# A transformer hybrid on one core: the first layer's shift vector summed on the tensor engine

## The chip, the core and the metric

The kernel runs on one core of a Trainium2 chip, as one launch. The metric is the device time of one execution in us. Matmuls run on the tensor engine (PE; its weight loads are the row PEld), elementwise work on the vector engine (DVE), activations and casts on ScalarE (ACT), small transfers and fills are issued by GpSimd (POOL), large transfers by SyncE (SP). SBUF is the working memory, PSUM holds the sums of the matmuls.

## The reference, cut to what matters

The network has 256 tokens of 1024 numbers, two layers of one kind (mixer, then a feed-forward or an expert stage) and two more of another. Each half of a layer begins with a normalised x, scaled and shifted by vectors which depend on one condition vector c alone. The change concerns the very first of these:

```python
def modulation(c, w, b):
    m = jnp.einsum("bd,de->be", jax.nn.silu(c), w) + b
    shift, scale, gate = jnp.split(m, 3, axis=-1)
    return shift[:, None], scale[:, None], gate[:, None]
...
    x = layer_norm(x, ln0_g, ln0_b)
    for layer in range(DEPTH):
        shift, scale, gate = modulation(c, ada_w[layer, 0], ada_b[layer, 0])
        ...
```

Shift, scale and gate are each a product of one row of 1024 numbers with a 1024 x 1024 matrix of float32, 4 MB from HBM.

## The kernel before

**Front.** Constants and x are loaded, x is normalised row by row in two tiles of 128 tokens (`layer_norm`, L436 to L448, mostly ScalarE, with short steps on the vector engine), and transposed by the tensor engine in blocks of 128x128 (`make_h`, L486). Meanwhile the modulation's first two vectors are made: `fill` takes them one after the other from a plan, scale first. `mod_rows` (L274) loads two row blocks of 128 x 1024 in one transfer of 1 MB and the vector engine multiplies each with its number of silu(c) per partition and adds it to a running tile `macc` (L292 for the first, L294 for the others): eight passes per vector. `mod_done` (L296) then sums `macc` over the partitions with eight matmuls against a column of ones (L171 is the line of the helper `mm`) and the vector engine adds the bias (L327). `ab` (L509) makes columns A and B of scale and shift with the first norm's gain and bias; ScalarE and the vector engine bring the transposed tokens through `x A + B` (L503, L501), cast them to their high part (L505) and take the rest as the low part (L506).

**Products.** Each product is made of three matmuls with exact high and low parts (L166, L167, L168). Weights come in blocks of 1 MB (`raw`, L119, issued by SP, four buffers), are cast by ScalarE (`hi`, L147) and subtracted on the vector engine (`lo`, L148). The first mixer begins with two projections (`proj_nat`, L605) and goes on with convolution, scan, attention, gating.

**What sets the order.** The program is written stage by stage; a scheduler places each engine's instructions in one fixed order, in which the engine then takes them, waiting at each for its inputs. A tile's buffer is taken again when its last reader is done: a transfer into one of the four `raw` buffers waits for that, and transfers issued behind it by SP wait with it.

**Small operands.** `setup` (L335) stacks vectors row by row into tiles (`stack`, transfers issued by POOL), transposes each stack on the tensor engine and copies it (`columns`, L379): col3 with the modulation's biases, col1 with the norms' gains, col2 and col4 with the rest.

## Time and profile before

| what | value |
|---|---|
| time, median of 3 runs | 2099.36 us (2097.38 to 2099.42) |
| span of the profiled execution, first to last instruction | 2100.0 us |
| its own time by the profile | the span: the page gives no other |
| busy: PE, PEld, DVE, ACT, POOL | 93%, 80%, 79%, 58%, 2% |
| mean granted clock of the tensor engine | 0.968 |
| HBM read, mean rate | 552.19 MB, 263 GB/s |

The shares are means over all stages. The front, in which the change lies, is 45 us of the span, and there the tensor engine is mostly idle. A timeline row gives start, duration, engine, line, operation, result and operands, how many instructions were merged into the row, and in brackets how long the engine was idle before and what ended it.

### The profile page before, as it was taken

What the parts mean: (1) busy time and instruction counts of PE and PEld (TensorE: products, weight loads), DVE (VectorE), ACT (ScalarE), POOL (GpSimd) and SP (SyncE); (2) the same over time, 40 slices, a digit from 0 to 9 for tenths busy, and PEclk for the clock granted to TensorE, in tenths of its full rate; (3) what the DMA queues carried; (4) which work ended last, traced back from release to release, by engine and by line L of the source; (5) the groups of instructions that cost most, each with busy time, mean ns of one, the idle gap of its engine ahead of it and who ended that gap; (6) DMA issues with size and microseconds to landing.
All of it is one profiled execution on the core that took longest, in us unless ns stands there. A gap on an engine that the chain in (4) does not pass through costs nothing.

```text
span 2100.0 us, 30041 instructions
## 1 busy us (share of the span) xinstructions
PE 1959.5 (93%) x11481; PEld 1681.4 (80%) x11481; DVE 1658.0 (79%) x2512; ACT 1208.3 (58%) x1817; POOL 50.1 (2%) x98
## 2 busy tenths in 40 slices
PE   3998999898599999999999999969989999998999
PEld 3887999886478787878778887858869998978998
DVE  6888977897588888888888888889778877667554
ACT  3454444452378767767776777755454446545442
POOL 4000000100000000000000000000000000000000
PEclk9999999998599999999999999979999999999999
DMA  9585998565489999899989999958339894326662
GB/s 319 181 287 202 339 331 308 177 224 204 141 300 360 328 339 334 317 358 346 340 322 348 344 360 351 360 181 278 124 132 346 322 320 147 121 87 214 203 199 80
DMA packets 283238, 555.25 MB, mean 264 GB/s; under 512 B 10172, under 2 KB 137520, under 8 KB 283088
## 3 DMA queue, kind: packets, MB, share of 16 engines
q1 hardware_dynamic: 280000, 549.49, 74.6%
q0 software_dynamic: 2656, 3.20, 0.8%
q8 instruction: 91, 1.49, 0.3%
q10 hardware_dynamic: 432, 0.58, 0.1%
q14 instruction: 59, 0.48, 0.1%
HBM read 552.19 MB, written 1.05 MB: 263 GB/s over the span
## 4 chain that ended last, share of the span: by engine, by line
PE 64%; DVE 5%; ACT 2%; issue 1%; DMA 1%; ACTq 0%; DVEq 0%
PE pp L167 12%; PE pp L168 11%; PE pp L166 11%; PE pa L634 6%; PE ya L167 4%; PE ya L166 4%; PE ya L168 4%; PE pp L175 3%; PE pj L166 1%; PE pj L167 1%; PE pj L168 1%; PE pp L171 1%; DVE lo L148 1%; PE sa L171 1%; ACT hi L147 1%
## 5 line engine op out<-in xcount | busy, mean ns | idle before, releaser
L148 DVE TENSOR_TENSOR lo<-raw,hi 128x1024 fp32r<-128x1024 f32 x660 | 787.5, 1220 | 193.1 <-ACT hi L147 191.5
L147 ACT CAST hi<-raw 128x1024 fp32r<-128x1024 f32 x660 | 668.4, 1051 | 393.6 <-PE pp L167 157.9
L166 PE MATMUL pp<-h,hi 128*128 128x256 f32 x960 | 274.4, 286 | 0.0
L168 PE MATMUL pp<-h,lo 128*128 128x256 f32 x960 | 271.6, 283 | 0.0
L167 PE MATMUL pp<-h,hi 128*128 128x256 f32 x960 | 271.5, 283 | 0.0
L148 DVE TENSOR_TENSOR lo<-rawx,hi 128x1024 fp32r<-128x1024 f32 x176 | 208.5, 1220 | 42.4 <-ACT hi L147 42.3
L294 DVE SCALAR_TENSOR_TENSOR macc<-raw,const,macc 128x1024 f32<-128x1024 f32 x168 | 215.3, 1281 | 6.6 <-DMA raw<-in_ada_w_dram 2.3
L167 PEld LDWEIGHTS pp<-h,hi 128*128 128x128 f32 x960 | 184.1, 192 | 1.9 <-issue 1.2
L166 PEld LDWEIGHTS pp<-h,hi 128*128 128x128 f32 x960 | 184.0, 192 | 1.8 <-ACT hi L147 1.0
L168 PEld LDWEIGHTS pp<-h,lo 128*128 128x128 f32 x960 | 184.1, 192 | 0.0
L147 ACT CAST hi<-rawx 128x1024 fp32r<-128x1024 f32 x176 | 176.5, 1048 | 11.9 <-PE pp L168 9.9
L166 PE MATMUL pj<-hi,h 128*128 128x256 f32 x576 | 169.6, 295 | 8.2 <-ACT h L505 3.7
L167 PE MATMUL pp<-lo,h 128*128 128x512 f32 (+1 forms) x480 | 174.6, 364 | 1.2 <-DVE lo L148 1.0
L166 PE MATMUL pp<-hi,h 128*128 128x512 f32 (+1 forms) x480 | 173.0, 361 | 0.0
L167 PE MATMUL pj<-lo,h 128*128 128x256 f32 x576 | 166.0, 290 | 0.8 <-DVE lo L148 0.8
L168 PE MATMUL pj<-hi,h 128*128 128x256 f32 x576 | 165.9, 290 | 0.0
L634 PE MATMUL pa<-hi,s 128*128 128x512 f32 x528 | 151.5, 396 | 0.0
L167 PE MATMUL pp<-lo,xe 128*128 128x512 f32 (+1 forms) x384 | 146.5, 382 | 1.3 <-DVE lo L148 1.0
L166 PE MATMUL pp<-hi,xe 128*128 128x512 f32 (+1 forms) x384 | 145.2, 379 | 0.0
L168 PE MATMUL pp<-hi,xe 128*128 128x512 f32 (+1 forms) x384 | 144.7, 377 | 0.0
L168 PE MATMUL pp<-hi,x 128*128 128x512 f32 (+1 forms) x384 | 143.2, 373 | 0.0
L167 PE MATMUL ya<-lo,s 128*128 128x512 f32 x352 | 141.9, 403 | 0.0
(481 smaller groups left out, 3563.3 us busy)
## 6 DMA issues: line engine op xcount, KB each, us to landing
raw<-in_moe_w_dram SPq DMA_DIRECT2D x176, 1024.0 KB, 6.1
rawx<-in_moe_w_dram SPq DMA_DIRECT2D x88, 1024.0 KB, 6.5
raw<-in_ada_w_dram SPq DMA_DIRECT2D x48, 1024.0 KB, 6.9
raw<-in_w_mod_dram SPq DMA_DIRECT2D x48, 1024.0 KB, 6.3
raw<-in_w_in_dram SPq DMA_DIRECT2D x42, 1024.0 KB, 5.8
raw<-in_ffn_w_dram SPq DMA_DIRECT2D x33, 1024.0 KB, 6.1
raw<-in_w_gate_dram SPq DMA_DIRECT2D x22, 1024.0 KB, 5.4
raw<-in_w_up_dram SPq DMA_DIRECT2D x22, 1024.0 KB, 5.5
```

Source lines behind the costliest of these rows:

```text
L147: self.nc.scalar.copy(h, v[:, z:z + m])
L148: self.nc.vector.tensor_tensor(l, v[:, z:z + m], h.bitcast(F32), ALU.subtract)
L166: mm(out, lhsT=a[0], rhs=b[0], start=start, stop=False)
L167: mm(out, lhsT=a[0], rhs=b[1], start=False, stop=False)
L168: mm(out, lhsT=a[1], rhs=b[0], start=False, stop=stop)
L171: self.nc.tensor.matmul(out, lhsT=lhsT, rhs=rhs, start=start, stop=stop)
L175: self.nc.tensor.transpose(out, in_, self.ident[:p, :p])
L294: V.scalar_tensor_tensor(acc, v[:, i], c, acc, ALU.mult, ALU.add)
L634: mm(accs[t][h], lhsT=y[ia][:, s], rhs=W[ib][:, h * 512:(h + 1) * 512], start=start and ia == 0 and ib == 0, stop=stop and ia == 1)
```

## The change

The shift vector of the first layer no longer goes over the vector engine. A new function `mod_first` loads its row blocks by turns with the scale's; each 128x128 piece of a shift block is the stationary operand of a matmul with one moving column, silu(c) for that row block, and all sums stay in one PSUM tile, which a matmul with zeros has opened. The last two row blocks of the shift come in transfers of their own, with the scale's sum between them. Around it: the gain columns col1 are made in the middle of `mod_first`, all other setup columns after `make_h` of the first step (in a PSUM pool of that stage; the stacks now have tiles of their own); the transposes of the first step are given a higher priority in the scheduler; the first gate's blocks are issued after the last matmul of the second projection. Comments and docstrings were also removed, which moves line numbers.

```diff
     def mm3(self, out, a, b, start, stop):
-        mm = self.nc.tensor.matmul
+        mm = self.mm_
...
+    def mm_(self, *args, **kw):
+        self.pe_last = self.nc.tensor.matmul(*args, **kw)
...
                 if key in self.gates_pe:
-                    self.mod_gate_pe(key)
+                    with self.tc.issue_after(self.pebar):
+                        self.mod_gate_pe(key)
...
+    def mod_first(self, scale, shift, setup):
+        w, b, j, c0 = self.mod_src(shift)
+        wv = w.rearrange("(k p) n -> p k n", p=128)
+        p = self.ps()
+        self.mm(p[:, 0:KD], self.zero, self.zero[:, 0:KD], True, False)
+        def shift_rows(k0, n):
+            v = self.raw(wv[:, k0:k0 + n, j * D:(j + 1) * D])
+            for i in range(n):
+                c = self.csil[:, c0 + k0 + i:c0 + k0 + i + 1]
+                for q in range(KD):
+                    self.mm(p[:, q:q + 1], v[:, i, q * 128:(q + 1) * 128], c, False, k0 + i == KD - 1 and q == KD - 1)
+        for k in range(0, KD, 2):
+            self.modpos = k
+            self.mod_rows(scale)
+            if k < 6:
+                shift_rows(k, 2)
+            else:
+                shift_rows(k, 1)
+                next(setup)
+                self.mods[scale] = self.mod_done(scale)
+                shift_rows(k + 1, 1)
+        c = self.tl("col", [128, KD])
+        q = ((shift[0] * 2 + shift[1]) * 3 + j) * KD
+        self.nc.vector.tensor_tensor(c, p[:, 0:KD], self.col3[:, q:q + KD], ALU.add)
+        self.mods[shift] = c
...
-            r = self.sc([128, 128])
+            r = self.tl("const", [128, 128], tag="r" + tag)
...
-            p = self.ps()
+            p = self.ps(pool="pp" if "pp" in self.pools else "sd")
...
         self.col1 = columns("col1", *r1)
+        yield
         self.col2 = columns("col2", r2, q)
...
-                for j in range(4):
-                    k = q + j
-                    self.tr(p[:, j], xn[:, t, k * 128:(k + 1) * 128])
+                with self.tc.high_priority(offset=400) if self.step == 1 else nullcontext():
+                    for j in range(4):
+                        k = q + j
+                        self.tr(p[:, j], xn[:, t, k * 128:(k + 1) * 128])
...
         p1 = self.proj_nat(h, w, 1448)
+        self.pebar = self.pe_last.ins
...
-            self.mod_start(plan[0])
+            self.mod_start([])
             x = self.load_x(a["x"])
             xn = x = self.layer_norm(x)
-            self.fill(KD * KD)
-            for _ in setup:
-                pass
+            self.mod_first((0, 0, SC), (0, 0, SH), setup)
...
                     h = self.make_h(xn, A, B)
+                    for _ in setup:
+                        pass
```

On the tensor engine, between the first transposes of the tokens and the first product, stood before (x_149 are the normalised tokens, const_103 the unit matrix, const_105 the ones, macc_204 and macc_232 the running tiles of scale and shift, sh_119, sh_126 and sh_144 the stacks col1, col2, col4; a row counts matmuls as they were written; each one-column matmul of float32 is two passes in the trace):

```order
L175 MATMUL pa_343<-const_103,x_149 128x128 x4
L175 MATMUL pa_355<-const_103,x_149 128x128 x4
L175 MATMUL pa_367<-const_103,x_149 128x128 x4
L171 MATMUL pp_222<-const_105,macc_204 128x1 x8
L171 MATMUL pp_250<-const_105,macc_232 128x1 x8
L175 MATMUL pp_260<-const_103,sh_119 128x112
L175 MATMUL pp_264<-const_103,sh_126 128x94
L175 MATMUL pp_268<-const_103,sh_144 128x96
L175 MATMUL pa_379<-const_103,x_149 128x128 x4
L166 MATMUL pj_423<-hi_415,h_341 128x256
```

and stands now (const_111 is silu(c), pp_204 the shift's sums, the raw tiles its row blocks, const_119, const_126 and const_144 the stacks):

```order
L178 MATMUL pp_287<-const_103,const_119 128x112
L178 MATMUL pa_374<-const_103,x_149 128x128 x4
L178 MATMUL pa_386<-const_103,x_149 128x128 x4
L174 MATMUL pp_204<-const_111,raw_211 128x1 x16
L178 MATMUL pa_398<-const_103,x_149 128x128 x4
L174 MATMUL pp_204<-const_111,raw_233 128x1 x16
L174 MATMUL pp_204<-const_111,raw_255 128x1 x16
L174 MATMUL pp_204<-const_111,raw_277 128x1 x8
L174 MATMUL pp_292<-const_105,macc_206 128x1 x8
L174 MATMUL pp_204<-const_111,raw_302 128x1 x8
L178 MATMUL sd_422<-const_103,const_126 128x94
L178 MATMUL sd_426<-const_103,const_144 128x96
```

The two sums of eight matmuls have become five groups of 16 or 8 for the shift with the scale's sum before the last of them; three of the four groups of transposes keep their place ahead, col1 moved ahead of them all, and the other stacks behind the sums.

On the vector engine, at the start, stood before (const_272 and const_274 are constants, const_117 is col3, t_150 to t_153 belong to the first token tile's mean and variance):

```order
L400 CAST const_272<-const_103 128x128
L403 CAST const_274<-const_103 128x128
L379 COPY const_117<-pp_115 128x96
L404 CAST const_274<-const_103 128x128
L443 TENSOR_SCALAR t_151<-t_150 128x1
L445 TENSOR_SCALAR t_153<-t_152 128x1
```

and stands now (const_430 is such a constant, const_289 is col1):

```order
L434 CAST const_430<-const_103 128x128
L412 COPY const_117<-pp_115 128x96
L412 COPY const_289<-pp_287 128x112
L477 TENSOR_SCALAR t_151<-t_150 128x1
L479 TENSOR_SCALAR t_153<-t_152 128x1
L185 TENSOR_SCALAR t_159<-t_153 128x1
```

The copy of col1 from pp_287 came in between col3 and the first step of the mean (t_151).

On ScalarE, from the end of the normalisation to the casts of the second or first weight block, stood before (hi_415 and hi_419 are the first block's halves; dc and h tiles are the tokens' parts, pa the transposes):

```order
L448 ACTIVATE x_149<-x_146,t_181,t_200 128x1024
L147 CAST hi_415<-raw_413 128x1024
L147 CAST hi_419<-raw_413 128x1024
L503 ACTIVATE dc_344<-pa_343,col_338,col_336 128x128 x3
L503 ACTIVATE dc_356<-pa_355,col_338,col_336 128x128 x2
L505 CAST h_341<-dc_344 128x4x128
L503 ACTIVATE dc_356<-pa_355,col_338,col_336 128x128
L503 ACTIVATE dc_368<-pa_367,col_338,col_336 128x128 x3
L505 CAST h_341<-dc_356 128x4x128
L503 ACTIVATE dc_380<-pa_379,col_338,col_336 128x128
L505 CAST h_341<-dc_368 128x4x128
```

and stands now (hi_465 and hi_469 are the first block's halves):

```order
L482 ACTIVATE x_149<-x_146,t_181,t_200 128x1024
L538 ACTIVATE dc_375<-pa_374,col_369,col_367 128x128 x3
L538 ACTIVATE dc_387<-pa_386,col_369,col_367 128x128 x2
L540 CAST h_372<-dc_375 128x4x128
L538 ACTIVATE dc_387<-pa_386,col_369,col_367 128x128
L538 ACTIVATE dc_399<-pa_398,col_369,col_367 128x128 x3
L540 CAST h_372<-dc_387 128x4x128
L538 ACTIVATE dc_411<-pa_410,col_369,col_367 128x128
L540 CAST h_372<-dc_399 128x4x128
L538 ACTIVATE dc_411<-pa_410,col_369,col_367 128x128 x2
L147 CAST hi_465<-raw_463 128x1024
L540 CAST h_372<-dc_411 128x4x128
```

The first weight block's two casts went from ahead of the tokens' steps to behind most of them.

## Rows read from the trace of the kernel before

**Rows 1.** The page's chain that ended last, share of the span by engine
```profile
PE 64%; DVE 5%; ACT 2%; issue 1%; DMA 1%; ACTq 0%; DVEq 0%
```

**Rows 2.** Waits of the tensor engine, 45 to 185 us; us in total, times, longest
```profile
PE pp L175 <- DVE x L562: 3.7, 1, 3.7
PE pp L175 <- ACT x L558: 3.1, 1, 3.1
```

**Rows 3.** Timeline of the front (start, us, engine, line, operation, count)
```profile
1.45 0.63 POOL L259 DMA_DIRECT2D gate<-in_ada_b_dram  x1
...
4.60 0.50 POOL L370 DMA_DIRECT2D sh<-in_norm_ffn_dram  x1
...
6.84 0.42 PE L175 MATMUL pp<-const,sh 96*128 96x96 f32 x1 [1.93 <-DMA sh<-in_ada_b_dram]
...
7.30 0.26 DVE L379 COPY const<-pp 128x96 f32<-128x96 f32 x1 [2.56 <-PE pp L175]
...
7.61 0.15 DVE L443 TENSOR_SCALAR t<-t 128x1 f32<-128x1 f32 x1
...
12.40 1.97 PE L175 MATMUL pa<-const,x 128*128 128x128 f32 x8 [5.14 <-ACT x L448]
...
26.24 0.74 DVE L292 TENSOR_SCALAR macc<-raw,const 128x1024 f32<-128x1024 f32 x1
...
27.02 9.21 DVE L294 SCALAR_TENSOR_TENSOR macc<-raw,const,macc 128x1024 f32<-128x1024 f32 x7
...
33.59 1.99 ACT L147 CAST hi<-raw 128x1024 fp32r<-128x1024 f32 x2 [12.40 <-DMA raw<-in_w_in_dram]
...
36.28 3.57 PE L171 MATMUL pp<-const,macc 128*128 128x1 f32 x16 [10.16 <-DVE macc L294]
...
42.42 0.16 DVE L521 TENSOR_TENSOR col<-col,col 128x8 f32<-128x8 f32 x1
```

**Rows 4.** Timeline at the first token tiles and products, 42 to 50 us
```profile
42.67 1.85 ACT L503 ACTIVATE dc<-pa,col,col 128x128 f32<-128x128 f32 x5 [7.09 <-DVE col L521]
...
45.10 0.57 PE L166 MATMUL pj<-hi,h 128*128 128x256 f32 x1
...
46.83 0.41 PE L166 MATMUL pj<-hi,h 128*128 128x256 f32 x1
...
47.04 0.41 PE L167 MATMUL pj<-lo,h 128*128 128x256 f32 x1
...
48.31 0.28 PE L167 MATMUL pj<-lo,h 128*128 128x256 f32 x1
...
48.35 1.10 ACT L147 CAST hi<-raw 128x1024 fp32r<-128x1024 f32 x1
...
48.43 0.28 PE L168 MATMUL pj<-hi,h 128*128 128x256 f32 x1
...
49.48 1.23 DVE L148 TENSOR_TENSOR lo<-raw,hi 128x1024 fp32r<-128x1024 f32 x1 [0.52 <-ACT hi L147]
```

**Rows 5.** Timeline of the tensor engine in the routing stage
```profile
548.96 6.84 PE L171 MATMUL pp<-sh,h 128*128 128x8 f32 x32
```

**Rows 6.** Timeline of the tensor engine where one-column and 256-column passes alternate
```profile
140.35 0.28 PE L171 MATMUL pa<-const,macc 128*128 128x1 f32 x2
...
140.70 0.28 PE L171 MATMUL pa<-const,macc 128*128 128x1 f32 x2
```

**Rows 7.** Stretches: busy us of PE, PEld, DVE, ACT, POOL; PEclk, DMA, GB/s
```profile
544.00:548.00 4.00, 2.11 (x12) 1.23 (x10) 4.00 (x5) 3.52 (x6) 0.00 (x0) 0.83 1.02 336
548.00:552.00 4.00, 3.95 (x19) 3.95 (x20) 2.22 (x3) 0.64 (x2) 0.00 (x0) 0.50 0.87 276
552.00:556.00 4.00, 3.80 (x18) 3.70 (x18) 0.16 (x1) 0.00 (x0) 0.00 (x0) 0.50 0.54 216
```

**Rows 8.** DMA issues, 0 to 60 us: count, KB each, us to landing
```profile
raw<-in_ada_w_dram SPq DMA_DIRECT2D x10, 1024.0 KB, 7.4
...
sh<-in_norm_ffn_dram POOLq DMA_DIRECT2D x1, 8.0 KB, 6.2
```

More of the change, by code (lines that the diff above doesn't have):

```diff
@@ L1499, in run @@
         plan = {
-            0: [(0, 0, SC), (0, 0, SH)],
             1: [(0, 0, GA), (0, 1, SC), (0, 1, SH)],
```

## The prediction

> **What bounds the kernel now.** I read the page first. The tensor engine holds 64% of the chain that ended last, the vector engine 5% [rows 1]. So the question is only when the tensor engine gets its first real product, and whether a delay there can be won back. The waits of the tensor engine from 45 to 185 us, the whole first mixer, answer the second half: two waits of 3.7 and 3.1 us, both at the layer's end, on its own results [rows 2]. From the first product on, the engine is never held by anything that a later start would not hold later too. So each us by which the first product starts later goes to the end, and each us earlier is won.
>
> Then I read the timeline of the front [rows 3]. The vector engine adds up the shift's rows in eight passes, the last seven of which run from 27.02 to 36.23 us; the tensor engine sums over partitions in 16 passes of one column from 36.28 for 3.57 us; columns A and B are done with the step at 42.42. ScalarE starts on the transposed tokens at 42.67 and the first product at 45.10 [rows 4]. ScalarE had waited for nothing to cast the first weight block: it did so at 33.59 [rows 3].
>
> **Part one: the vector engine loses eight passes, the tensor engine gets 128.** The shift's product has eight row blocks of 128 and eight columns of 128 each: 64 matmuls with one moving column. In float32 one such matmul is two passes, as the 16 passes for eight matmuls show [rows 3]. So 128 passes are added, each with its own load of a 128x128 block. Those removed from the vector engine lay on the path (36.23 - 26.24 = 10.0 us) [rows 3]; the 16 passes of the shift's old sum (3.57) go too.
>
> What is one pass worth? At half clock: the 32 passes with eight moving columns from 548.96 take 6.84 us, 0.214 each [rows 5]; the one-column row gives 3.57/16 = 0.223 with its tail [rows 3]. At full clock: between 140.35 and 140.70 stand two one-column passes and one of 256, so about 0.115 each [rows 6]. Which clock will it be? In the first 48 us the clock column of the profile shows 1.00, but the spacing contradicts it: at 46.83 and 47.04 passes stand 0.21 apart, at 48.31 and 48.43 0.12 [rows 4]. So the tensor engine starts at 1.2 GHz, and goes over to 2.4 only behind its first 256-column passes. Narrow passes don't seem to do this: while the stream at 548.96 ran without a gap, the granted clock was 0.50 in both 4 us stretches, with weight loads busy for 3.95 and 3.70 of 4 us, and it had been higher before (0.83) [rows 5, 7]. I take 0.214.
>
> The Trainium skill ("TensorE: Matmul & The Clock Gate", Part 1) says that the throttled state is the default and sustained matmul activity releases it; by that rule the gapless stream here would go over to full clock by itself, which is the second case below. The trace disagrees for narrow passes: 6.84 us of them stayed at 0.50.
>
> **Part two: when the stream can begin.** On the tensor engine the first shift block stands behind the transposes of token tile 0, which start at 12.40 when the normalised tile is there [rows 3]. Eight at 0.214 end at 14.1. But the normalisation itself is pushed back. The vector engine's copy of the stacked gain columns now stands ahead of its first mean step, which ran at 7.61. That copy needs six transfers issued by POOL, the last at 4.60, landing 6.2 later, 10.8 [rows 3, 8]. POOL has the gate's transfer (1.45) and some memsets fewer ahead of them, so about 1.0 earlier: 9.8. Transpose and copy took from 6.84 to 7.56 for the other stack; the mean step then comes at 10.2 to 10.5, 2.6 to 2.9 late. Bounds: 0 (the transfers land in time) and 3.8 (no earlier than before). I take 2.6. The stream starts at 16.7.
>
> **Part three: the stream.** The order is: shift rows 0 and 1 (32 passes), four transposes of tile 1, rows 2 and 3 (32), rows 4 and 5 (32), row 6 (16), the scale's sum (16), row 7 (16). That is 148 passes, 31.7 us: it ends at 48.4, if every block is there. Blocks take turns in four buffers. Rows 4 and 5 need the buffer that rows 0 and 1 free at 23.5; with 7.4 us to landing [rows 8] they are there at 30.9, wanted at 31.2. Row 6 is issued at 31.2, there by 38.6, wanted at 38.1. The scale's last block is queued on SP right behind rows 4 and 5 and lands about 3 us after them, 34; two vector passes make it 37, wanted at 41.5. So the transfers cost nothing or 0.5 us. The vector engine's long stretch vanishes, and the tensor engine is late in its place.
>
> From the end of the sum to ScalarE it took 42.67 - 39.85 = 2.8 us before, with column copies and a weight's low part between. These now stand behind, and four short steps remain: about 0.7. ScalarE starts at 49.1, which is 6.4 later than 42.67.
>
> **Part four: the first weight's casts lose their cover.** Before, ScalarE cast the first weight block while it waited, and the vector engine made the low parts around the column steps. Now both stand behind the four tiles of tokens: ScalarE's first cast has the place of the second block's first cast (48.35, done 49.45, that is 6.8 after ScalarE's start), and the vector engine's low part that at 49.48, done 8.0 after the start [rows 4]. The first product needs the one, the second pass the other. Before, the first product came 2.4 after ScalarE's start, and pass 15 5.4 after it. Now pass 2 comes at 8.1 and pass 15 at 8.1 + 13 x 0.214 = 10.9, since the engine is cold again. That is 5.4 us more, 4 if it should be warm, 7 if it rises later. What follows keeps up: each weight needs two casts of 1.1 us on ScalarE [rows 4] for 48 passes of the tensor engine.
>
> The move of the other setup columns, the tensor engine's gate blocks (kept behind the second projection, where they stood) and the tile pools I put at nothing: behind the first products the tensor engine's order is the old one but for a few swapped neighbours. The two copies and five small steps for the setup columns, about 1.1 us on the vector engine, now stand ahead of its first step on the tokens; ScalarE's five steps on the tokens (1.85) [rows 4] hide them, and without that cover they would cost up to 1.1.
>
> **Sum.** 6.4 + 5.4 = 11.8 us. The profiled execution's span of 2100.0 is 0.6 over the median of the timed runs, 2099.36, so the difference carries over unchanged: 2099.4 + 11.8 = 2111.2. Own range of this case: 2107 (normalisation not late, clock soon up) to 2116 (transfers a little late, clock later).
>
> **The rivals.** First, the one that ends on the other side: the clock goes up in the narrow stream. For it speaks that the stream is nearly five times as long as any narrow one in this trace; against it the 0.50 in both stretches [rows 7]. Passes then cost 0.115, and the blocks decide. With half of the first 32 passes still slow, rows 0 and 1 end at 22.0; rows 4 and 5 land 7.4 later, 29.4, and are summed by 33.1; row 6, the scale and row 7 are 48 passes, 5.5, to 38.6. ScalarE starts at 39.3, 3.4 earlier than before, and the casts take back 4 to 5.4, which is 2100 to 2101; with blocks that land 3 us sooner in the emptier queue it is 2097 to 2098. I take 2099, no change: even then the casts eat the gain. This case decides once the stream is done by about 38 instead of 48.
>
> Second, the transfers hold the stream. Each next shift block is issued only when a pair has left its buffer. If landing took 10 us instead of 7.4, rows 4 and 5, row 6 and the following block would each be some 2 us late: about 2117. Against it: 7.4 is the median with the queue full, and here at most two are under way.
>
> Third, the change does not do what it says on the path: the lag is won back in the mixer, where the vector engine now has fewer halves in arrears. Then only the 6.4 is left, or less: 2105. Rows 2 speak against it.
>
> **How the numbers follow.** First case 0.78, at 2111; clock up 0.09, at 2099; transfers 0.06, at 2117; won back 0.07, at 2105. The range, 2103 to 2116, leaves out the clock's case and most of the transfers' one, and holds the whole own range of the first case. What a measurement can tell from no change is 0.2%, 4.2 us: faster means under 2095.2, for which only a clock that is up from the first block would do: 0.03. Same is the rest of the clock's case and the better half of the won-back one: 0.10. Slower: 0.87.
>
> **What would show it.** In the new profile: the one-column passes 0.21 apart, the stream from about 17 to 48 us without gaps; the mean step of the normalisation near 10; ScalarE's start on the tokens near 49; its first weight cast behind them and the first 256-column product near 56. I am wrong if the passes stand 0.12 apart, if the tensor engine waits for blocks for several us, or if the first product is late by 12 and the end is not.

## The result: 0.6% slower, by the steps that were predicted

The changed kernel takes 2112.01 us (median of four runs, 2111.24 to 2112.82), the kernel before, in four runs beside it, 2099.14 (2097.38 to 2099.42). The ratio is 1.0064, with a 95% interval of 1.0049 to 1.0078: 12.9 us, where 11.8 were predicted. The profiled execution took 2112.55 us, of which 2110.8 are the span.

Busy time in the kernel before (first line) and in the changed one, and the changed kernel's chain of waits that ended last, which answers to [rows 1]:

```profile
PE 1959.5 (93%) x11481; PEld 1681.4 (80%) x11481; DVE 1658.0 (79%) x2512; ACT 1208.3 (58%) x1817; POOL 50.1 (2%) x98
...
PE 1982.0 (94%) x11594; PEld 1704.3 (81%) x11594; DVE 1650.9 (78%) x2504; ACT 1208.7 (57%) x1817; POOL 50.7 (2%) x98
...
PE 63%; DVE 5%; ACT 2%; issue 1%; DMA 1%; ACTq 0%; DVEq 0%
```

The vector engine is busy for 7.1 us less, and the kernel is slower: the vector engine has 5% of the chain in both, the tensor engine 64 and 63%. The timeline of the changed front, with the columns of [rows 3, 4], has every step of the prediction in it:

```profile
10.54 0.28 DVE L412 COPY const<-pp 128x112 f32<-128x112 f32 x1 [3.11 <-PE pp L178]
...
10.73 0.14 DVE L477 TENSOR_SCALAR t<-t 128x1 f32<-128x1 f32 x1
...
17.28 6.83 PE L174 MATMUL pp<-const,raw 128*128 128x1 f32 x32
...
24.85 17.07 PE L174 MATMUL pp<-const,raw 128*128 128x1 f32 x80
...
41.78 3.55 PE L174 MATMUL pp<-const,macc 128*128 128x1 f32 x16
...
45.19 3.55 PE L174 MATMUL pp<-const,raw 128*128 128x1 f32 x16
...
49.40 1.86 ACT L538 ACTIVATE dc<-pa,col,col 128x128 f32<-128x128 f32 x5 [27.89 <-DVE col L556]
...
55.09 1.10 ACT L147 CAST hi<-raw 128x1024 fp32r<-128x1024 f32 x1
...
56.24 0.58 PE L171 MATMUL pj<-hi,h 128*128 128x256 f32 x1 [4.07 <-ACT hi L147]
...
57.50 0.58 PE L171 MATMUL pj<-lo,h 128*128 128x256 f32 x1 [0.68 <-DVE lo L148]
...
60.44 0.63 PE L171 MATMUL pj<-hi,h 128*128 128x256 f32 x2
...
62.15 0.41 PE L171 MATMUL pj<-lo,h 128*128 128x256 f32 x1
...
62.67 0.28 PE L171 MATMUL pj<-lo,h 128*128 128x256 f32 x1
```

The reader is to see four things. The gains' copy at 10.54 holds the mean step behind it (10.73; 7.61 before). The stream of narrow passes goes from 17.28 to 48.74, with four transposes of the second token tile in it, at 17.07/80 = 0.213 us a pass. ScalarE starts on the tokens at 49.40 (42.67 before) and comes to the first weight's cast only at 55.09. And the first product at 56.24 still runs at the lower clock: 0.41 us for the 256-column matmul at 62.15, 0.28 for the one at 62.67.

The tensor engine never waited in the stream: it is busy for the whole of every stretch of 4 us from 18 to 46 us. Two of them (columns as in [rows 7]) show this, and once more that the clock column can't be trusted at the start: it says 1.00 over passes that stand 0.21 us apart.

```profile
22.00:26.00 4.00, 4.00 (x21) 4.00 (x21) 3.25 (x3) 0.00 (x0) 3.71 (x7) 1.00 0.56 96
...
38.00:42.00 4.00, 4.00 (x21) 4.00 (x20) 0.00 (x0) 0.00 (x0) 0.00 (x0) 1.00 0.61 189
```

Was anything won back? The waits of the tensor engine from 56 to 198 us, the same piece of the program as in [rows 2]:

```profile
PE pj L171 <- ACT hi L147: 4.1, 1, 4.1
PE pp L178 <- DVE x L597: 3.7, 1, 3.7
PE pp L178 <- ACT x L593: 3.3, 1, 3.3
PE pj L171 <- DVE lo L148: 0.7, 1, 0.7
```

The two waits at the layer's end are those of before (3.7 and 3.1 there); the two new ones are those ahead of the first and the second product. As a landmark for the end of the first mixer I take ScalarE's first step on the second step's tokens: 180.09 us before, 192.86 after. The lag there is 12.8 us. Between the medians of the timed runs it is 12.9.

The spans of the two profiled executions differ by less, 2110.8 - 2100.0 = 10.8. Their lag is 13.9 us still at ScalarE's weight cast at 545.52 of the kernel before and 9.1 at the one at 580.97. In between, in the routing stage, the granted clock rose sooner in the changed kernel's execution; here the kernel before, then the same piece of the changed kernel 13 us later:

```profile
570.00:580.00 10.00, 8.88 (x39) 7.66 (x40) 3.47 (x7) 6.95 (x14) 0.00 (x0) 0.67 0.00 0
...
583.00:593.00 10.00, 9.01 (x49) 7.24 (x48) 5.85 (x9) 8.05 (x15) 0.00 (x0) 1.00 0.00 0
```

The profiled execution of the kernel before was also one of its longer ones. Its time is not given; in the profiled executions of all other runs the time is 1.75 to 2.15 us more than the span, so it took some 2102 us, an estimate, where the median is 2099.14. One pair of traces can't tell whether the change has a part in that stage. The medians give no sign that anything is won back behind the first mixer.

### The profile page after: what moved, and what is told of

It is laid out like the page before. It is cut to its first block, busy times and chain, and to the rows that moved or that the text cites. A ratio compares the mean times of both kernels' runs of the same rounds, so it can differ in the third digit from the quotient of the medians.

```text
span 2110.8 us, 30245 instructions
## 1 busy us (share of the span) xinstructions
PE 1982.0 (94%) x11594; PEld 1704.3 (81%) x11594; DVE 1650.9 (78%) x2504; ACT 1208.7 (57%) x1817; POOL 50.7 (2%) x98
## 4 chain that ended last, share of the span: by engine, by line
PE 63%; DVE 5%; ACT 2%; issue 1%; DMA 1%; ACTq 0%; DVEq 0%
PE pp L171 34%; PE ya L171 11%; PE pa L669 6%; PE pj L171 4%; PE pp L178 3%; DVE lo L148 1%; PE sa L174 1%; PE pp L174 1%; ACT hi L147 1%; PE sb L174 1%; PE pa L174 1%; PE sb L669 1%; DMA raw<-in_w_in_dram 1%; PE pj L669 0%; ACT s L1193 0%
## 5 line engine op out<-in xcount | busy, mean ns | idle before, releaser
L171 PE MATMUL pp<-h,hi 128*128 128x256 f32 x1920 | 349.3, 284 | 0.0
L171 PEld LDWEIGHTS pp<-h,hi 128*128 128x128 f32 x1920 | 300.4, 192 | 3.7 <-ACT hi L147 1.2
L171 PE MATMUL pj<-hi,h 128*128 128x256 f32 x1152 | 229.5, 295 | 11.7 <-ACT hi L147 4.1
L171 PE MATMUL ya<-hi,s 128*128 128x512 f32 x704 | 231.3, 397 | 0.0
L171 PE MATMUL pp<-hi,xe 128*128 128x512 f32 (+1 forms) x768 | 228.3, 376 | 0.0
L298 DVE SCALAR_TENSOR_TENSOR macc<-raw,const,macc 128x1024 f32<-128x1024 f32 x161 | 206.3, 1282 | 20.1 <-DMA raw<-in_ada_w_dram 12.5
L171 PEld LDWEIGHTS pj<-hi,h 128*128 128x128 f32 x1152 | 188.7, 198 | 16.6 <-ACT hi L147 4.5
L171 PE MATMUL pp<-hi,h 128*128 128x512 f32 (+1 forms) x576 | 183.3, 352 | 0.0
L171 PEld LDWEIGHTS pp<-hi,xe 128*128 128x128 f32 x768 | 139.8, 188 | 27.8
L171 PEld LDWEIGHTS ya<-hi,s 128*128 128x128 f32 x704 | 132.1, 188 | 29.1
```

The lines of the kernel that those rows point to most:

```text
L171: self.pe_last = self.nc.tensor.matmul(*args, **kw)
L298: V.scalar_tensor_tensor(acc, v[:, i], c, acc, ALU.mult, ALU.add)
```

## The experiments

Each was timed in 4 to 12 executions, beside runs of the kernel before on the same chip. In the edits `issue_after(x)` gives an instruction a place behind x in its engine's order. "Tokens" is ScalarE's first step on the transposed tokens, "product" the first 256-column matmul, "mixer" the landmark above, all three in us of the profiled execution.

| run | time | before, beside it | ratio, 95% interval | tokens | product | mixer |
|---|---|---|---|---|---|---|
| before | | 2099.14 | | 42.67 | 45.10 | 180.09 |
| changed kernel | 2112.01 | 2099.14 | 1.0064 (1.0049 to 1.0078) | 49.40 | 56.24 | 192.86 |
| e1_gain_late | 2110.13 | 2101.03 | 1.0045 (1.0033 to 1.0058) | 46.70 | 53.53 | 189.71 |
| e2_cast_ahead | 2109.48 | 2101.03 | 1.0038 (1.0025 to 1.0051) | 49.24 | 53.58 | 188.84 |
| e3_both | 2104.79 | 2101.03 | 1.0023 (1.0014 to 1.0031) | 46.36 | 50.69 | 185.36 |
| e5_shift_vector | 2109.06 | 2101.03 | 1.0038 (1.0025 to 1.0051) | 47.66 | 50.87 | 189.44 |
| e8_vector_no_wait | 2105.74 | 2099.85 | 1.0035 (1.0022 to 1.0049) | 45.34 | 48.55 | 187.00 |
| e4_wide_between | 2112.49 | 2099.85 | 1.0058 (1.0044 to 1.0071) | 48.30 | 55.14 | 191.54 |
| e10_wide_turns | 2121.45 | 2100.03 | 1.0103 (1.0089 to 1.0118) | 50.08 | 56.91 | 193.74 |
| e7_vector_all_edits | 2102.36 | 2099.85 | 1.0011 (1.0001 to 1.0021) | 42.85 | 47.18 | 181.88 |
| e6_split | 2102.59 | 2099.85 | 1.0017 (1.0008 to 1.0026) | 43.69 | 48.02 | 183.76 |
| e9_split_mask | 2099.87 | 2100.03 | 0.9999 (0.9990 to 1.0008) | 42.25 | 44.67 | 180.28 |
| e11_vector_mask | 2099.50 | 2100.03 | 1.0000 (0.9990 to 1.0011) | 41.16 | 43.58 | 178.38 |
| e12_vector_late_loads | 2097.98 | 2099.90 | 0.9988 (0.9979 to 0.9997) | 40.00 | 42.42 | 178.19 |

An interval is some 2 to 3 us wide to each side. Between runs of neighbouring size the landmark of the trace therefore tells more than the time, though it is one execution each. In all runs but the one with forced turns (e10) the landmark's lag and the difference of the two times agree within 1.6 us.

### The gains' copy, and the casts: one by one, then both

```diff
             c = self.tl("const", [128, q], tag=tag)
-            V.tensor_copy(c, p[:, 0:q])
+            with self.tc.issue_after(self.last.ins) if tag == "col1" else nullcontext():
+                V.tensor_copy(c, p[:, 0:q])
```

> The changed kernel, with one instruction moved: VectorE's copy of the layer norm's gains (L412, 128x112) is issued behind the last rsqrt step of the normalisation instead of ahead of its first mean step. Theory (the copy makes the normalisation late, and the tensor engine's stream starts after it and lasts its own 31.5 us): the mean step runs at about 7.6 us instead of 10.73, the stream starts at about 14.2 instead of 17.28, ScalarE starts the tokens at about 46.3 instead of 49.4, and the time falls by 3.1 us to about 2109.0. Rival (the stream is held by its transfers, so an earlier start only opens gaps in it): the stream starts earlier but ends near 48.7 all the same, ScalarE at 49.4, time within 0.5 us of 2112.0.

```diff
-                    h = self.make_h(xn, A, B)
+                    if s == 1:
+                        self.w0 = self.wcol(a["w_in"][0], 1280)
+                    with self.tc.issue_after(self.cast.ins) if s == 1 else nullcontext():
+                        h = self.make_h(xn, A, B)
```

> The changed kernel, with ScalarE's casts of the first weight block (L147, two) and VectorE's subtractions behind them put ahead of the token steps, as they stood by themselves in the kernel before. Theory (of the 12.8 us that the first mixer ends late, about 6 are the casts that lost their cover and the clock that then rises later): ScalarE starts the tokens near 49.4 as before the edit, the first product comes at about 52 instead of 56.2, the clock rises about 4 us sooner, and the time falls by 5 to 6 us to about 2106.5. Rival (the casts are hidden and the loss after 49.4 is the low clock alone, which needs its own stretch of products): first product as early, but less than 2 us of it is left at the end, about 2110 or more.

> Both edits at once (gains' copy behind the normalisation, first casts ahead of the token steps). Theory: the two losses are separate terms of one chain and add: 3.1 + 5.5 = 8.6 us less than the changed kernel, about 2103.5, still some 4 us above the kernel before because the 31.5 us stream itself remains. Rival (both gains end in the same wait): the better of the two alone, about 2106.5.

The copy's price is what was said: without it the stream starts at 13.54 and ScalarE at 46.70, and the mixer ends 3.15 us sooner. The time is 9.1 us above the kernel before, where the changed kernel's is 12.9. The stream from 13.54 to 46.05 is 1.0 longer than in the changed kernel, of which 0.73 is a wait for the second token tile; none is for a block, so the transfers did not hold it. Timeline of that run:

```profile
13.54 6.98 PE L174 MATMUL pp<-const,raw 128*128 128x1 f32 x32
...
46.70 1.85 ACT L539 ACTIVATE dc<-pa,col,col 128x128 f32<-128x128 f32 x5 [25.50 <-DVE col L557]
```

With the casts ahead the mixer ends 4.02 sooner, not 5.5. The time is 8.5 us above the kernel before, 4.4 less than the changed kernel's, where 5 to 6 were expected. The product came at 53.58, 1.6 later than I expected, and the timeline of that run says why: ScalarE casts in good time, but the two subtractions behind the casts now stand ahead of the vector engine's step on the tokens, and ScalarE waits for that.

```profile
43.58 1.99 ACT L147 CAST hi<-raw 128x1024 fp32r<-128x1024 f32 x2 [22.50 <-DMA raw<-in_w_in_dram]
...
50.08 2.35 DVE L148 TENSOR_TENSOR lo<-raw,hi 128x1024 fp32r<-128x1024 f32 x2
...
52.78 0.62 ACT L540 CAST h<-dc 128x512 fp32r<-128x512 f32 x1 [1.35 <-DVE dc L536]
...
53.58 0.56 PE L171 MATMUL pj<-hi,h 128*128 128x256 f32 x1
```

Both edits together give 7.50 at the landmark; the sum of the two is 7.17. The time is 3.8 us above the kernel before, as expected. So they are separate terms of one chain, and both rivals (the transfers, one common wait) fall. What is left, 5.3 us, is the stream and the order that came with it: ScalarE starts at 46.36, 3.7 later than before, and from there to the first product it takes 1.9 longer, behind the two subtractions.

### The engine choice alone

The shift's blocks go back to the vector engine, by turns with the scale's, the last two in one transfer again; everything else stays as changed.

```diff
-                    self.mm(p[:, q:q + 1], v[:, i, q * 128:(q + 1) * 128], c, False, k0 + i == KD - 1 and q == KD - 1)
...
+            for key in (scale, shift):
...
+                self.modpos = k
+                self.modacc = acc.get(key)
+                self.mod_rows(key)
+                acc[key] = self.modacc
...
+        for k in range(KD):
+            self.mm(p[:, k:k + 1], acc[shift][:, k * 128:(k + 1) * 128], self.ones[:, 0:1])
```

> The changed kernel with the engine choice alone undone: the shift's eight row blocks are loaded by turns with the scale's as in the changed kernel, but summed on VectorE into a second accumulator, and the tensor engine sums over partitions in 16 passes at the end; the 128 narrow passes per block row are gone, the gains' copy stays where the change put it. Theory (the narrow stream at 0.214 us a pass is the main loss): ScalarE starts the tokens at about 41 to 45 us instead of 49.4 and the time is 2102 to 2106. Rival (the order of the loads, not the engine, makes it late: the turns and the later normalisation cost the same on VectorE): ScalarE near 49 and time within 1 us of 2112.

This missed: 2109.06, above the upper end of 2106. But the edit had brought a wait of its own. The scale's column step stood ahead of the shift's last two passes on the vector engine, as this row of its timeline shows:

```profile
40.70 0.17 DVE L331 SCALAR_TENSOR_TENSOR col<-pp,const 128x8 f32<-128x8 f32 x1 [3.73 <-PE pp L174]
```

So it was run again with that step behind the last pass (an `issue_after` around `mod_done`).

> The run before that put the shift's blocks back on VectorE had an added wait of 3.7 us: the scale's column step stood ahead of the shift's last two passes and waited there for the tensor engine. Here it stands behind them; gains' copy and casts as in the changed kernel. Theory (with that wait gone, what is left of the difference to the changed kernel is the engine choice): VectorE's passes end at about 39.6 instead of 43.4, ScalarE starts the tokens at about 44 instead of 47.7, and the time is 3.7 us less than that run's, about 2105.5 (some 5 us above the kernel before). Rival (the transfers set VectorE's last pass, not the wait): ScalarE still near 47, time within 1 us of that run's 2109.1.

The time, 2105.74, is as expected. ScalarE's start, 45.34, is 1.3 later than expected: the passes wait 2.94 us for a block and end at 40.25 (39.6 expected), and on the tensor engine the shift's sum now stands right behind the scale's.

```profile
34.98 5.26 DVE L298 SCALAR_TENSOR_TENSOR macc<-raw,const,macc 128x1024 f32<-128x1024 f32 x4 [2.94 <-DMA raw<-in_ada_w_dram]
...
37.74 6.95 PE L174 MATMUL pp<-const,macc 128*128 128x1 f32 x32 [13.46 <-DVE macc L298]
...
45.34 1.85 ACT L533 ACTIVATE dc<-pa,col,col 128x128 f32<-128x128 f32 x5 [3.63 <-DVE col L551]
```

The engine choice is worth 4.1 us at ScalarE's start and 5.9 at the landmark, of 12.8; not all of the 5.9 is the stream, because one of the first two casts also came ahead of the tokens in this order. Of the other 6.9 us, 5.1 go with the gains' copy and the casts put back as well (e7_vector_all_edits below), which hang on the order and not on the engine; the last 1.8 go once the mask is cleared first and the first weight's subtractions are moved (e11_vector_mask).

### Is it the clock that sets a pass's 0.214 us?

```diff
+        wide, fill = self.ps(), self.zero.unsqueeze(1).to_broadcast([128, 3, 128])
+        for _ in range(6):
+            self.mm(wide[:, 0:384], self.zero, fill)
...
                     self.mm(p[:, q:q + 1], v[:, i, q * 128:(q + 1) * 128], c, False, k0 + i == KD - 1 and q == KD - 1)
+                    self.mm(wide[:, 0:384], self.zero, fill)
```

> The changed kernel with work added on the tensor engine and nothing else: a 384-column bf16 product of zeros (into a PSUM tile that nothing reads) behind each of the stream's 64 one-column matmuls, and six of them ahead of the stream. Theory (the passes are 0.214 us apart because the clock stays at its lower level, and the narrow passes are what keeps it there): with wide products between them the clock goes up early in the stream, a matmul's two passes take 0.23 us and a filler 0.16, 64 times 0.39 is 25 us beside 27.4 for the 128 passes alone, the sum ends at about 45 in spite of the added work, the first weight's products then start at the higher clock, and the time is some 4 to 8 us below the changed kernel's, 2104 to 2108. Rival (0.214 us is what loading a 128x128 fp32 block of raw takes at any clock, so that the fillers only add): the sum ends 10 to 21 us later, near 60 to 70, and the time is 2122 to 2133.

Neither time came: 2112.49, 12.6 us above the kernel before, as the changed kernel. The scheduler had put 49 of the 70 wide products ahead of the first narrow matmul and the others in clumps, so that this run is not the one I meant. For the question it is the better one, because it has long runs of narrow passes alone, behind wide ones. Two rows of its timeline, the passes that ran from 30 to 34 and from 36 to 40 us:

```profile
29.78 4.38 PE L174 MATMUL pp<-const,raw 128*128 128x1 f32 x38
...
35.78 4.41 PE L174 MATMUL pp<-const,raw 128*128 128x1 f32 x20
```

and its stretches there (columns as in [rows 7]):

```profile
30.00:32.00 2.00, 2.00 (x20) 2.00 (x20) 1.96 (x2) 0.00 (x0) 0.00 (x0) 1.00 0.56 109
32.00:34.00 2.00, 2.00 (x20) 2.00 (x20) 0.31 (x1) 0.00 (x0) 0.00 (x0) 1.00 1.03 422
34.00:36.00 2.00, 2.00 (x14) 2.00 (x13) 1.30 (x2) 0.00 (x0) 0.00 (x0) 0.61 0.97 375
36.00:38.00 2.00, 2.00 (x11) 2.00 (x11) 1.27 (x1) 0.00 (x0) 0.00 (x0) 0.50 0.35 143
```

The same pass takes 4.38/38 = 0.115 us at a granted 1.00 and 4.41/20 = 0.22 at 0.50. It is not the transfers: the slow stretch from 36 has the smallest DMA share of the four, and the fast one from 32 the largest. So the pass follows the clock, and a stream of narrow passes alone, that began at 28.86 at the higher level, was at the lower one by 36. At ScalarE's start 1.1 us came back. More did not: the tensor engine never stood still from 18 to 46 us, but the two clumps behind the first 32 passes took 5.5 us of it (22.34 to 26.45 and 27.49 to 28.86), and from 36 on the passes were slow again.

```diff
...
                 for q in range(KD):
-                    self.mm(p[:, q:q + 1], v[:, i, q * 128:(q + 1) * 128], c, False, k0 + i == KD - 1 and q == KD - 1)
+                    with self.tc.issue_after(self.turn.ins):
+                        n = self.nc.tensor.matmul(p[:, q:q + 1], lhsT=v[:, i, q * 128:(q + 1) * 128], rhs=c,
+                                                  start=False, stop=k0 + i == KD - 1 and q == KD - 1)
+                    with self.tc.issue_after(n.ins):
+                        self.turn = self.nc.tensor.matmul(wide[:, 0:384], lhsT=self.zero, rhs=fill, start=True, stop=True)
```

> In the run with wide products the order on the tensor engine put nearly all of them ahead of the narrow matmuls instead of between them: there the clock was at the higher level when the narrow passes began (about 0.11 us a pass) and fell back while they ran alone (0.214 from about 35 us on). Here each of the 64 one-column matmuls is held behind the 384-column bf16 product before it, so that they do take turns; six products stand ahead. Theory (narrow passes alone let the clock fall, wide ones among them hold it up): after a first few turns at 0.76 us (two passes at 0.214 and a filler at 0.33) a turn takes 0.40, the sum ends at about 47 (48.7 in the changed kernel) in spite of 64 fillers, and the granted clock stays at 1.00 to the end of it. Rival (it was something else that slowed the passes, such as the transfers into raw beside them): turns stay at 0.76, the sum ends near 70, and the time is 2130.

In the trace the first half of the theory holds. Stretches of that run, each turn being three instructions:

```profile
24.00:28.00 4.00, 4.00 (x40) 3.83 (x39) 0.29 (x1) 0.00 (x0) 1.75 (x6) 1.00 0.94 311
28.00:30.00 2.00, 0.10 (x2) 0.03 (x1) 0.00 (x0) 0.00 (x0) 0.00 (x0) 1.00 1.07 365
30.00:32.00 2.00, 2.00 (x20) 2.00 (x21) 0.00 (x0) 0.00 (x0) 0.00 (x0) 1.00 0.88 123
32.00:34.00 2.00, 2.00 (x15) 2.00 (x14) 0.00 (x0) 0.00 (x0) 0.00 (x0) 0.55 0.97 367
```

At the higher clock a turn with its added product takes 0.30 us (40 instructions in 4 us), less than the two passes alone at the lower one (0.43). The work then runs ahead of its transfers: from 28 to 30 the tensor engine waits 1.9 us for a block. The clock reads 0.55 in the stretch from 32 to 34 and 0.50 from there to the end of the sum at 49.4, in the same mix (the scale's sum apart) that had run at 1.00; why it fell no run here shows. So the second half of the theory fails. The time is 2121.45, 9 us above the changed kernel. The profiled execution took 2113.25 and the three others 2120 to 2123; why those are longer no trace shows, and it stays open.

### A version that beats both?

Three of the shift's blocks on the tensor engine, or none, with both orders mended:

```diff
+                if k + i in on_pe:
+                    for q in range(KD):
+                        self.mm(p[:, q:q + 1], v[:, i, q * 128:(q + 1) * 128], cc, False, False)
+                elif first:
+                    V.tensor_scalar(sacc, v[:, i], cc, None, ALU.mult)
...
+                else:
+                    done = V.scalar_tensor_tensor(sacc, v[:, i], cc, sacc, ALU.mult, ALU.add)
```

> As the run with the shift on VectorE and no added wait, with the gains' copy behind the normalisation and the first casts ahead of the token steps as well. Theory (everything that the turns themselves can give without the tensor engine): VectorE's passes run back to back from 11 us, ScalarE starts the tokens at about 39.5 (42.67 in the kernel before), and the time is 1 us below the kernel before, between 3 below and 2 above. Rival (the order of the loads by turns costs as such): ScalarE at 43 or later, 3 us or more above the kernel before.

> A version meant to beat both: of the shift's eight row blocks the tensor engine sums three (0, 1, 2: 48 narrow passes, 10 us at the lower clock) and VectorE five into an accumulator whose sum over partitions is added in the same PSUM tile; the scale stays on VectorE; gains' copy behind the normalisation, first casts ahead of the token steps. Theory (each engine gets what it can do while the transfers run): VectorE's 13 passes end at about 31, ScalarE starts the tokens at about 35 (42.67 before, 49.4 after the change), the first product comes at about 39.5 (45.1 before) and the time is 6 us below the kernel before, 3 to 8. Rival (the first mixer waits for its own weights next, whose transfers come after the sixteen blocks): ScalarE starts as early but the gain ends in waits for the weights' transfers, within 2 us of the kernel before.

Both theories fell: 2102.36 and 2102.59, above the kernel before. ScalarE started at 42.85 and 43.69, where 39.5 and 35 were expected; the first comes near its rival without reaching it, the second to neither. The timeline of the split version shows a wait that is only 1.3 us long in the changed kernel, where the stream covers it. The attention mask is cleared by GpSimd (L445 there), and the change moved that behind 24 small transfers that GpSimd issues; in the vector engine's queue the mask's cast stands between the second token tile's first steps.

```profile
17.92 0.44 POOL L445 MEMSET const<- 128x384 bf16 x1
...
18.39 0.23 DVE L446 CAST const<-const 128x128 bf16<-128x128 f32 x1 [4.93 <-POOL const L445]
...
33.39 2.60 DVE L298 SCALAR_TENSOR_TENSOR macc<-raw,const,macc 128x1024 f32<-128x1024 f32 x2 [3.22 <-DMA raw<-in_ada_w_dram]
...
39.09 1.99 ACT L147 CAST hi<-raw 128x1024 fp32r<-128x1024 f32 x2 [17.48 <-DMA raw<-in_w_in_dram]
```

The passes behind it free the buffers late, the next blocks come late, and the first weight too. Two more versions clear the mask first and put the first weight's subtractions into the vector engine's wait for the sums:

```diff
         nc.gpsimd.memset(self.zero, 0.0)
+        self.maskb = self.tl("const", [128, 384], BF16, tag="maskb")
+        nc.gpsimd.memset(self.maskb, 0.0)
...
+        self.w0 = self.wcol(self.a["w_in"][0], 1280)
...
+        with self.tc.issue_after(self.sub.ins):
+            self.nc.vector.tensor_tensor(c, p[:, 0:KD], self.col3[:, q:q + KD], ALU.add)
```

> The version with three of the shift's blocks on the tensor engine and five on VectorE lost its lead in three waits that its trace shows: VectorE stood from 13.4 to 18.4 us for GpSimd's clearing of the mask (L445, at 17.92, behind GpSimd's 24 DMA issues; in the kernel before at 1.02), ahead of the second token tile's normalisation and of all passes behind it; the blocks' transfers, held by the buffers that VectorE had not freed, came late, and the first weight's too (39.1 instead of 33.6); and ScalarE stood 1.35 us for VectorE's token step behind two subtractions. Here the mask is cleared first on GpSimd, and the two subtractions stand in VectorE's wait for the shift's sums. Theory (these are the waits): no gap on VectorE at 13 to 18, its last pass ends at about 34 instead of 38.6, ScalarE starts the tokens at about 38.5 (42.67 in the kernel before), the first product comes at about 42 (45.1) and the time is 3 us below the kernel before, 1 to 5. Rival (the transfers are the bound from here on): VectorE's last pass still ends at 37 or later, and the time is within 1 us of the kernel before or above it.

> The same without the tensor engine's part: all eight of the shift's blocks on VectorE, by turns with the scale's, gains' copy behind the normalisation, mask cleared first, the first weight's subtractions in VectorE's wait. Theory (VectorE's sixteen passes, 20 us, are then the bound, from 11 us with 3 us of normalisation between them): last pass at about 35, ScalarE at about 39.5, and the time 2 us below the kernel before, that is within 1 us of the version with the tensor engine's three blocks, which therefore gain nothing. Rival (the transfers set the last pass): VectorE waits for raw and ends at 37 or later as before, time at or above the kernel before.

The gap at 13 to 18 us is gone, and both are level with the kernel before. Both rivals hold in the main: the vector engine's last pass still ends at 37.9 and 36.9, and it waits for blocks. One row of the split version's timeline (its waits for blocks add up to 9.2 us):

```profile
27.06 2.61 DVE L363 SCALAR_TENSOR_TENSOR macc<-raw,const,macc 128x1024 f32<-128x1024 f32 x2 [2.65 <-DMA raw<-in_ada_w_dram]
```

and one stretch of the version without the tensor engine, with the DMA engines fully busy at 297 GB/s:

```profile
22.00:26.00 4.00, 0.00 (x0) 0.00 (x0) 3.43 (x4) 0.00 (x0) 2.39 (x5) 1.00 1.04 297
```

In that stretch GpSimd issues the mixer's small weights in short pieces, which stood at 40.75 before the change. The last run holds them:

```diff
         wq = [self.tl("w", [128, 4, 128]) for _ in range(2)]
+        if self.step == 1:
+            for k in range(2):
+                V.tensor_copy(wq[k][:, 0, 95:113], self.first.to_broadcast([128, 18]))
```

> The version with all of the shift on VectorE and the mask cleared first, once more, with GpSimd's loads of the mixer's small weights (L760 of that version's trace, 18.2 to 26 us, 64-byte to 384-byte pieces) held until the shift vector is there, as they stood in the kernel before (40.75); two copies of 18 columns on VectorE hold them. Theory (from 18 us on the block's and first weight's transfers share the DMA engines with these loads: 230 to 345 GB/s at a full DMA share where it was 400): the first weight's cast starts near 35 instead of 37.1, VectorE's last pass ends near 35 instead of 36.9, the tokens start near 39.5 instead of 41.2, and the time is 1.5 us less than that version's, 2 us below the kernel before. Rival (the buffers that VectorE frees, not the DMA engines, set the transfers): VectorE's last pass still ends at 36.5 or later, time as that version's, within 1 us of the kernel before.

The timeline of that run:

```profile
35.19 1.99 ACT L148 CAST hi<-raw 128x1024 fp32r<-128x1024 f32 x2 [16.96 <-DMA raw<-in_w_in_dram]
...
40.05 4.47 POOL L764 DMA_DIRECT2D w<-in_mla_w_qb_dram  x6 [17.81 <-DVE col L556]
...
42.42 0.57 PE L172 MATMUL pj<-hi,h 128*128 128x256 f32 x1
```

The front has the theory's numbers: the cast at 35.19, the last pass done at 34.8, the first product at 42.42, 2.7 before that of the kernel before. The time is 1.9 us below it, the landmark 1.9 too: faster, though by 0.12% (0.03 to 0.21), less than a single comparison is sure of. What the held loads alone gave is less sure: against the run before this one the first product comes 1.2 sooner, the landmark only 0.2, and the intervals of the two times overlap. The theory's reason shows only in part: from 18 to 30 us the DMA engines moved 354 GB/s, in the run before 345, and from 22 to 26 no more than there:

```profile
22.00:26.00 4.00, 0.00 (x0) 0.00 (x0) 2.40 (x2) 0.00 (x0) 0.24 (x1) 1.00 1.02 255
26.00:30.00 4.00, 0.00 (x0) 0.00 (x0) 2.97 (x3) 0.00 (x0) 0.00 (x0) 1.00 1.02 411
```

Of the change this version has the turns of the loads and the new places of small steps, and nothing on the tensor engine.

## Why the prediction was right

**What bounds the kernel.** The claim that each us of the first product's delay goes to the end held: 11.1 us at the product, 12.8 at the first mixer's end, 12.9 between the medians of the times (10.8 between the two profiled spans, for the reason above). Of the 1.6 us between the first two, 0.9 is the longer way from the first to the second pass (1.26 us, 0.36 before), the rest the clock that rose later. The rival "won back in the mixer" is out. One step of the sum was a slip without effect: it set the span of the profiled execution, 2100.0, beside the median of the times, though the span leaves out some 2 us that a time has.

**Part one, the narrow passes.** 0.214 was taken, 0.213 measured, over 128 + 16 passes and four transposes without a gap. That it is the clock's lower level was shown in one run on the same passes (0.115 at 1.00). The Trainium skill ("TensorE: Matmul & The Clock Gate", Part 1) says that sustained matmul activity releases the throttle; 31 us of gapless narrow passes did not, so the trace disagrees for this kind of activity, and the rival that rested on that rule is out. What that rival said of a faster stream, that then the blocks decide, was seen: with forced turns at the higher clock the stream waited 1.9 us for a block.

**Part two, the normalisation.** Predicted 2.6 late; the mean step came 3.1 late (10.73) and the stream 0.6 later than said (17.28 for 16.7). Moving the copy alone gave 3.15 back.

**Part three, the stream and its transfers.** 31.7 us predicted, 31.5 measured (17.28 to 48.74). I had counted on 7.4 us to landing. In the changed kernel the median of the seven 1 MB blocks is 10.6, but that is the length of the queue at the start and of the scale's last block. The two blocks that could hold the stream were there sooner than worked out: rows 4 and 5, issued at 24.14, in 5.2 us, at 29.3 for passes that begin near 31.7, and row 6, issued at 31.71, in 6.1. The issue of rows 4 and 5, and the transfers of these two blocks with columns as in [rows 8]:

```profile
24.14 0.37 SPq L119 DMA_DIRECT2D raw<-in_ada_w_dram  x1
...
raw<-in_ada_w_dram SPq DMA_DIRECT2D x1, 1024.0 KB, 5.2
...
raw<-in_ada_w_dram SPq DMA_DIRECT2D x1, 512.0 KB, 6.1
```

So the condition of the rival "transfers hold the stream", at 2117, did not come true, and the argument against it did: few blocks are under way by then. ScalarE started 6.7 later, 6.4 predicted.

**Part four, the casts.** 5.4 predicted, 12.77 - 6.73 = 6.04 measured. Pass 15 comes out as worked out: 57.50 + 13 x 0.214 = 60.3, seen at 60.44, 11.0 behind ScalarE's start. In the kernel before, though, it stands at 48.43 [rows 4], 5.8 behind ScalarE's start and not 5.4, so that up to there the delay is 5.3. Then the clock stayed low until 62.4, some nine passes more at 0.214 in place of 0.115, 0.9 us. It rose 4.9 us behind the second pass, in the kernel before 2.9 (45.46, the row below, to 48.3 in [rows 4]).

```profile
45.46 0.41 PE L167 MATMUL pj<-lo,h 128*128 128x256 f32 x1
```

I had named this case, at 7. So the working was right, and its two small errors partly cancel, which is luck. By the experiment 4.0 of the 6.0 come back with the casts' place alone.

**What I put at nothing.** The moved mask was in fact free in the changed kernel, 1.3 us of idle vector engine under the stream, but only because the late normalisation and the stream covered it. With the gains' copy moved away (e1_gain_late) the vector engine already waits 4.7 us for it, and this is what makes the second token tile late there; in the split version it is 4.9. The prediction did not name it.

## What to carry to other kernels

Before moving a sum to an engine because that one is idle, price it at the clock that the engine has there: here 144 narrow passes in a row ran at the lower level to their end, and the first products behind them began at it. Of 12.8 us only about half hung on the engine; most of the rest was two changes of place, a copy ahead of a mean step and two casts behind the token steps, which the order of instructions shows before any run. And an edit at no cost is so by its cover: when the cover goes, look again for what is queued ahead.

## What the runs showed that I had not expected

- In these traces the granted clock reads 1.00 from the start until it first falls, in the changed kernel over passes that stand 0.213 us apart; the spacing of equal instructions is the better gauge there (0.22 against 0.115 us for a narrow pass).
- A mix of narrow and wide products ran at the higher clock from 18.4 to 32 us, the last 2 us of it behind a wait of 1.9 us for a block, and then at 0.55 and 0.50 with the mix unchanged; the wait as the cause is not shown.
- Without the tensor engine's stream the vector engine still waits for blocks in this front (3.7 us in e11, 2.6 in e12), and a full DMA share is not one rate: 297 GB/s from 22 to 26 us in e11, 255 in the same stretch of e12, 411 from 26 to 30 there.
- The same piece of the routing stage was 4.8 us shorter in the changed kernel's profiled execution than in that of the kernel before, over a granted clock that rose sooner: more than a third of the effect looked for, in a stage far behind the edit.
